# Scan loads of a hybrid encoder kernel: the shape of the DMA that fetches keys, gate rows, maxima and factors

## The chip, the cores and the metric

The kernel runs on one core of one Trainium2 chip. The metric is the device time of one execution in microseconds. The core has five engines with an instruction list each, worked through in order: PE (TensorE, matmuls; PEld is its weight load), DVE (VectorE), ACT (ScalarE), POOL (GpSimd) and SP (SyncE), which here issues nearly all DMAs. Sixteen DMA engines carry the transfers.

## What is computed

One layer of a bidirectional encoder on 2048 tokens of width 1024, in float32. Three head groups read one normalised input: neighbourhood attention (6 heads), mLSTM (4 heads of 64) and gated DeltaNet (6 heads of 64). The last two run in chunks of 64 tokens, forwards and backwards, each as a scan. Their outputs go through one projection; then follow cross-attention on 256 memory tokens, a squared-ReLU MLP and a last norm. What matters here are the two scans:

```python
# gated DeltaNet, per head and direction, chunk by chunk
def step(state, xs):
    u_c, w_c, a_c, qd_c, ks_c, gl_c = xs          # qd = q * exp(gc)
    v_new = u_c - w_c @ state
    o = qd_c @ state + a_c @ v_new
    state = state * exp(gl_c) + ks_c.T @ v_new
    return state, o

# mLSTM: m_t is the running maximum
s_intra = (q @ k.T) * exp(dmat - m_t)
a_inter = exp(inter - m_t)
num = a_inter * (q @ c_prev) + s_intra @ v
```

## The kernel before

`pass_a` projects the input and prepares the chunks: `gram` (L408) makes keys, decays and Gram matrices for 128 tokens at a time, `inv` inverts triangular blocks, `ml_prep` makes the mLSTM rows. What the scans need goes to DRAM: `kb_d` (keys times exp(gc), written at L471), `sc_d`, `v_d`, `w_d`, `gd_c`, `g_st` (cumulated gates, one row of 768 numbers for a step and direction), `mlc_d`, `mlv_d`, `mx_row` (running maxima, rows of 512) and `ai_row` (factors, rows of 512).

`pass_b` runs three generators side by side: `gdn_scan`, `ml_scan` one step later, and `heads_out`, which from the ninth mLSTM step on finishes two token tiles a step. Each scan has 16 steps of 128 tokens. A tile of 128 partitions holds both directions at once: partitions 0 to 63 and 64 to 127 (`CH`, and the swapped `SR`) belong to direction 0 at token tile m and to direction 1 at token tile 15 - m. All tiles of the scans have two buffers.

`load(m)` of `gdn_scan` (L625) fetches `wp`, `sc` (two transfers) and `qe` for each direction (L634 to L637) and then, for both directions in one transfer, `kb` (the keys) and `ge` (the gate row, the same 3 KB for each of 64 partitions), through `both` at L657. ACT takes the exponential of `ge` (L640), POOL multiplies `qe` by it into `sc` (L643), DVE writes the scaled identity into `sc` (L644), PE multiplies keys and inverses (L651), ACT copies that into `wp` (L654). A step of the scan itself is then a chain of matmul and copy: L674, L676, L681, L684, twice, with the outputs at L688 and L693 or L695.

`load(m)` of `ml_scan` (L829) fetches `mkq`, `mr_` and `mqe` by direction (L839 to L842) and, for both directions in one transfer each, `me` (the maxima, 2 KB for each of 64 partitions, L843) and `mge` (the factors, L844). DVE subtracts `me` (L845), POOL adds a mask (L846), ACT takes the exponential (L847), DVE uses it (L862); POOL uses `mge` (L866). L896 to L910 turn numerators and denominators into outputs.

In one transfer for both directions the source is a slice over the rows of a flattened (direction, token tile) axis: it takes row m and row 31 - m, so the first dimension of the source has 2 entries, and the second has 64 (rows of keys, or a repeat). The order on each engine is set by a scheduler in the framework, which plans with its own clock, so that a change of a DMA may reorder instructions near it. The names `mr__9279` and the like are the buffers of `mr_` by number.

Of the kernel before, what the change touches and what calls it, by code (L numbers as in the profile page):

```python
# [37 lines left out]
class Trunk:  # L38
# [59 lines left out]
    def mix(self):  # L98

        tc, nc, I, dr = self.tc, self.nc, self.I, self.dr  # L100
        dt = lambda name, shape: dr.tile(shape, F32, name=name)
        self.y_d = [dt(f"y_d{b}", [8, P, 512]) for b in range(4)]
        self.gd_c = dt("gd_c", [9, P, T])
        self.gate_d = dt("gate_d", [5, P, T])
        self.mlc_d = dt("mlc_d", [16, P, 4, P])
        self.mlv_d = dt("mlv_d", [16, P, 4, 65])
        self.nac_d = dt("nac_d", [6, P, T])
        self.nav_d = dt("nav_d", [T, 384])
        self.g_row = dt("g_row", [16, 2, 2, 6, 64])
        self.sc_d = dt("sc_d", [2, 16, 2, 64, 2, 6, 64])  # L110
        self.kb_d = dt("kb_d", [2, 16, 64, 2, 6, 64])
        self.g_st = dt("g_st", [2, 16, 2, 6, 64])
        self.v_d = dt("v_d", [16, 2, 64, 6, 64])
        self.x_d = dt("x_d", [384, 64, 64])
        self.w_d = [[dt(f"w_d{d}{g}", [64, 12 * (b - a), 64]) for g, (a, b) in enumerate(GROUPS)] for d in range(2)]
        self.wt_d = [dt(f"wt_d{d}", [192, 32, 32]) for d in range(2)]
        with ExitStack() as big:
            self.c = big.enter_context(self.pool("mixc", 1))
            c = self.c
            self.ind2 = self.load_const("ind2", [P, 2])  # L120
            self.gmask = self.load_const("gmask", [P, 2, 64])
            self.egl = c.tile([P, 4, 2, 2, 4, 6], F32, name="egl")
            self.rr = c.tile([P, 16, 12], F32, name="rr")
            self.gcm = c.tile([P, 2, 16, 4], F32, name="gcm")
            self.gtm = c.tile([P, 2, 16, 4], F32, name="gtm")
            self.cm = c.tile([P, 2, 16, 4], F32, name="cm")
            self.cmx = c.tile([P, 2, 16, 4], F32, name="cmx")
            self.wxx = c.tile([P, 2, 16, 4], F32, name="wxx")
            self.emt = c.tile([P, 2, 16, 4], F32, name="emt")
            self.pass_a()  # L130
            self.pass_b()
# [276 lines left out]
    def gram(self, t):  # L408

        nc, pool = self.nc, self.tp  # L410
# [3 lines left out]
        e = pool.tile([P, 2, 6, 64], F32, name="gr")  # L414
# [49 lines left out]
        for d in range(2):  # L464
            sc = pool.tile([P, 3, 6, 64], F32, name="sc")
            V.tensor_tensor(out=byp(sc[:, 0]), in0=gv[:, :, :, 0:64], in1=byp(e[:, d]), op=ALU.mult)
            V.tensor_tensor(out=sc[:, 1], in0=heads(kt), in1=col(kst[:, d]), op=ALU.mult)
            V.tensor_tensor(out=sc[:, 2], in0=heads(kt), in1=col(self.eg[:, t, d]), op=ALU.mult)
            nc.sync.dma_start(out=self.sc_d[d, t].rearrange("c s a h l -> (c s) (a h l)"), in_=sc[:, 0:2].rearrange("p a h l -> p (a h l)"))
            for c2 in range(2):  # L470
                nc.sync.dma_start(out=self.kb_d[d, t, :, c2], in_=sc[64 * c2:64 * c2 + 64, 2])  # L471

    def inv(self, g, dirs, late=False):

# [140 lines left out]
    def gdn_scan(self, pool):  # L615
# [4 lines left out]
        nc, dr = self.nc, self.dr  # L620
        V, G = nc.vector, nc.gpsimd
        CH = (slice(0, 64), slice(64, 128))
        SR = (slice(64, 128), slice(0, 64))

        def load(m):  # L625
            wp = pool.tile([P, 2, 2, 6, 64], F32, name="wp")
            sc = pool.tile([P, 2, 2, 3, 6, 64], F32, name="sc")
            kb = pool.tile([P, 2, 6, 64], F32, name="kb")
            ge = pool.tile([P, 2, 6, 64], F32, name="ge")
            qe = pool.tile([P, 6, P], F32, name="qe")  # L630
            for d in range(2):
                t = m if d == 0 else 15 - m
# [2 lines left out]
                nc.sync.dma_start(out=sc[CH[d], d, :, 0:2].rearrange("p c a h l -> p c (a h l)"), in_=self.sc_d[d, t].rearrange("c s a h l -> s c (a h l)"))  # L635
                nc.sync.dma_start(out=sc[CH[d], d, :, 2].rearrange("p c h l -> p c (h l)"), in_=self.v_d[t].rearrange("c s h l -> s c (h l)"))
                nc.sync.dma_start(out=qe[SR[d]], in_=self.gd_c[0:3, :, P * t:P * t + P].rearrange("c (h e) l -> e (c h) l", h=2))  # L637
            both(kb.rearrange("p c h l -> p (c h l)"), self.kb_d.rearrange("d t s c h l -> (d t) s (c h l)")[m:32 - m:31 - 2 * m])
            both(ge.rearrange("p c h l -> p (c h l)"), self.g_st.rearrange("d t c h l -> (d t) (c h l)")[15 - m:17 + m:2 * m + 1, None].broadcast_to([2, 64, 768]))
            nc.scalar.activation(out=ge, in_=ge, func=AF.Exp)  # L640
            for d in range(2):
                t = m if d == 0 else 15 - m
# [14 lines left out]
        def both(out, in_):  # L657

            nc.sync.dma_start(out=out, in_=in_)
# [6 lines left out]
        for m in range(16):  # L666
            nxt = load(m + 1) if m < 15 else None
            wp, sc = cur
# [148 lines left out]
    def ml_scan(self, pool):  # L817
# [11 lines left out]
        def load(m):  # L829
# [7 lines left out]
            for d in range(2):  # L837
# [2 lines left out]
                nc.sync.dma_start(out=r[CH[d], d].rearrange("p c h x -> p c (h x)"), in_=self.mlv_d[t].rearrange("(c s) h x -> s c (h x)", c=2))  # L840
                for a in range(2):
                    nc.sync.dma_start(out=qe[SR[d], a::2], in_=self.mlc_d[t, CH[a], 0:2])  # L842
            nc.sync.dma_start(out=e.rearrange("p c h l -> p (c h l)"), in_=self.mx_row.rearrange("d t c h l -> (d t) (c h l)")[m:32 - m:31 - 2 * m, None].broadcast_to([2, 64, 512]))  # L843
            nc.sync.dma_start(out=ge.rearrange("p h l -> p (h l)"), in_=self.ai_row.rearrange("d t h c l -> (d t) (h c l)")[15 - m:17 + m:2 * m + 1, None].broadcast_to([2, 64, 512]))  # L844
            V.tensor_tensor(out=e, in0=self.cmx[:, :, m, :, None].broadcast_to([P, 2, 4, 64]), in1=e, op=ALU.subtract)  # L845
            G.tensor_tensor(out=e, in0=e, in1=gm[:, None, None, :].broadcast_to([P, 2, 4, 64]), op=ALU.add)  # L846
            nc.scalar.activation(out=e, in_=e, func=AF.Exp)  # L847
# [564 lines left out]
```

## Time and profile before

| | us |
|---|---|
| median of the runs (2 runs, 4184.78 to 4187.43) | 4186.1 |
| the profiled execution | 4188.59 |
| its span, first to last instruction | 4186.8 |
| of it before the scans (0 to 985) | 985 |
| the scans (985 to 1752) | 767 |
| attention, projections, MLP (from 1752) | 2435 |

The scans' first loads are issued at about 955 us (mLSTM) and 992 us (DeltaNet); the last output tile of `heads_out` is done at 1752.03 us. PE is busy for 3492.6 us of the span (83%), DVE 1778.6, ACT 1120.4, POOL 1435.6. The granted TensorE clock is 0.903 of full speed in the mean, the lowest stretch being the scans. A stretch is read by the busy time of each engine, by who waits for what, and by the share of the 16 DMA engines that is busy.

### The profile page before, as it was taken

The page shows a single profiled execution, that of the slowest core. Times are in us where ns is not written, and L with a number is a line of the kernel's source. Part 1 is how long each engine was busy: PE and PEld are TensorE (multiplying, and loading weights), DVE is VectorE, ACT ScalarE, POOL GpSimd, SP SyncE. Part 2 cuts the span into 40 slices and gives each one's busy share as a digit, 9 for nine tenths or more (in the row PEclk, how much of TensorE's full clock was granted, in tenths as well). Part 3 has the DMA queues.
Part 4 walks back from the last instruction along what each step waited for, and adds up shares of the span by engine and source line. Part 5 has one row for each costly group of instructions (what it writes and reads, how often), then busy time and mean ns, then how long its engine had stood idle before and what let it go on. Part 6 is the DMA issues. An engine that isn't in the chain of part 4 may idle for free.

```text
span 4186.8 us, 53799 instructions
## 1 busy us (share of the span) xinstructions
PE 3492.6 (83%) x21360; PEld 2802.8 (67%) x21360; DVE 1778.6 (42%) x3241; ACT 1120.4 (27%) x1976; POOL 1435.6 (34%) x876
## 2 busy tenths in 40 slices
PE   5988999893233335499799999999999999999998
PEld 4766777673233334376578888778888877888887
DVE  7767483832133456644343434532222244222224
ACT  3222422231111111155343333422211133221122
POOL 4241523342121223211344534443333354333333
PEclk8999999895566667599899999999999999999999
DMA  4476435844243344345323233321111132111112
GB/s 132 112 212 130 137 87 168 221 105 116 89 99 94 102 116 118 134 129 158 114 86 126 96 119 131 106 78 43 46 48 48 56 101 83 43 43 48 51 51 86
DMA packets 375844, 425.24 MB, mean 102 GB/s; under 512 B 150872, under 2 KB 277544, under 8 KB 373544
## 3 DMA queue, kind: packets, MB, share of 16 engines
q1 hardware_dynamic: 375048, 420.22, 34.4%
q8 instruction: 169, 2.77, 0.3%
q0 software_dynamic: 544, 1.57, 0.2%
q14 instruction: 83, 0.68, 0.1%
HBM read 329.59 MB, written 92.12 MB: 101 GB/s over the span
## 4 chain that ended last, share of the span: by engine, by line
PE 54%; DVE 2%; issue 1%; ACT 1%; DMA 1%; POOL 1%; SPq 0%; POOLq 0%; DVEq 0%; ACTq 0%
PE psg L94 30%; PE psa L94 19%; PE psn L960 2%; PE psy L979 1%; PE pst L969 1%; DVE ss L1030 0%; PE psm L75 0%; PE psa L1198 0%; DMA xb<-x_d 0%; PE psm L85 0%; PE pst L986 0%; ACT whi L1001 0%; DMA me<-mx_row 0%; DVE gz L727 0%; POOL wlo L1003 0%
## 5 line engine op out<-in xcount | busy, mean ns | idle before, releaser
L1003 POOL TENSOR_TENSOR wlo<-wraw,whi 128x1024 fp32r<-128x1024 f32 (+2 forms) x386 | 774.4, 2007 | 1515.6 <-ACT whi L1001 1408.4
L94 PE MATMUL psg<-acta,whi 128*128 128x512 f32 (+1 forms) x3008 | 967.0, 402 | 22.4 <-ACT acta L1155 16.2
L94 PE MATMUL psg<-actb,whi 128*128 128x512 f32 x2496 | 796.5, 399 | 40.7 <-ACT actb L266 13.8
L1001 ACT CAST whi<-wraw 128x1024 fp32r<-128x1024 f32 (+2 forms) x402 | 357.6, 890 | 1217.1 <-PE psa L94 554.8
L94 PEld LDWEIGHTS psg<-acta,whi 128*128 128x128 f32 (+1 forms) x3008 | 569.4, 191 | 160.5 <-ACT acta L1155 17.5
L94 PE MATMUL psa<-ht,whi 128*128 128x512 f32 x2048 | 638.8, 395 | 0.6 <-ACT whi L1001 0.6
L94 PE MATMUL psg<-acta,wlo 128*128 128x512 f32 (+1 forms) x1504 | 602.3, 401 | 3.6 <-POOL wlo L1003 3.6
L94 PEld LDWEIGHTS psg<-actb,whi 128*128 128x128 f32 x2496 | 470.5, 190 | 156.3 <-ACT actb L266 14.6
L94 PE MATMUL psg<-actb,wlo 128*128 128x512 f32 x1248 | 499.5, 401 | 2.9 <-POOL wlo L1003 2.9
L94 PEld LDWEIGHTS psa<-ht,whi 128*128 128x128 f32 x2048 | 384.0, 188 | 94.1 <-ACT whi L1001 1.5
L94 PE MATMUL psa<-ht,wlo 128*128 128x512 f32 x1024 | 400.6, 396 | 0.5 <-POOL wlo L1003 0.5
L1247 DVE TENSOR_TENSOR fr<-fr 128x512 f32<-128x512 f32 x128 | 167.4, 1307 | 511.8 <-ACT fr L1246 511.8
L1260 DVE TENSOR_TENSOR xb<-psa,xb 128x512 f32<-128x512 f32 x256 | 175.8, 692 | 475.6 <-PE psa L94 475.6
L94 PEld LDWEIGHTS psg<-acta,wlo 128*128 128x128 f32 (+1 forms) x1504 | 286.8, 191 | 72.7 <-POOL wlo L1003 4.7
L94 PEld LDWEIGHTS psg<-actb,wlo 128*128 128x128 f32 x1248 | 236.5, 190 | 59.7 <-POOL wlo L1003 4.1
L1250 POOL TENSOR_TENSOR ht<-fr,ht 128x512 fp32r<-128x512 f32 x128 | 169.5, 1324 | 257.3 <-ACT ht L1249 254.2
L94 PEld LDWEIGHTS psa<-ht,wlo 128*128 128x128 f32 x1024 | 192.2, 188 | 48.4 <-POOL wlo L1003 1.7
L674 PE MATMUL pss<-sc,wp 128*64 128x64 f32 x768 | 48.1, 278 | 210.8 <-ACT sc L684 190.2
L674 PEld LDWEIGHTS pss<-sc,wp 128*64 128x64 f32 x768 | 40.7, 185 | 217.4 <-ACT sc L684 194.1
L681 PE MATMUL pss<-sc 128*64 128x64 f32 x744 | 53.8, 291 | 116.3 <-DVE sc L676 98.0
L301 DVE SCALAR_TENSOR_TENSOR acc<-pad,vecs,acc 128x512 f32<-128x512 f32 (+2 forms) x144 | 143.9, 1013 | 2.8
L1030 DVE TENSOR_TENSOR ss<-ss,sqt 128x512 f32<-128x512 f32 (+1 forms) x91 | 122.4, 1345 | 49.1 <-ACT sqt L1029 45.9
(383 smaller groups left out, 4141.9 us busy)
## 6 DMA issues: line engine op xcount, KB each, us to landing
wraw<-in_w_ff SPq DMA_DIRECT2D x72, 512.0 KB
wraw<-in_w_ff SPq DMA_DIRECT2D x144, 256.0 KB
wraw<-in_w_out SPq DMA_DIRECT2D x32, 512.0 KB
wraw<-in_w_xq SPq DMA_DIRECT2D x32, 512.0 KB
wraw<-in_w_xo SPq DMA_DIRECT2D x32, 512.0 KB
wraw<-in_w_gd SPq DMA_DIRECT2D x24, 512.0 KB
sc_d<-sc SPq DMA_DIRECT2D x32, 384.0 KB
sc<-sc_d SPq DMA_DIRECT2D x32, 384.0 KB
```

The source lines that it names most:

```text
L94: nc.tensor.matmul(out=out, lhsT=a(k), rhs=b(k), start=(i == 0), stop=(i == n - 1))
L301: V.scalar_tensor_tensor(out=acc[:, :n], in0=pad[:, p0 + j:p0 + j + n], scalar=cw(j), in1=acc[:, :n], op0=ALU.mult, op1=ALU.add)
L674: nc.tensor.matmul(out=ps[CH[d], 64 * h:64 * h + 64], lhsT=wp[:, d, cc[d], h], rhs=sc[:, d, cc[d], 2, h], start=True, stop=True)
L681: nc.tensor.matmul(out=ps[SR[d], 64 * h:64 * h + 64], lhsT=sc[:, d, cc[d], 1, h], rhs=sc[:, d, cc[d], 2, h], start=True, stop=True)
L960: nc.tensor.matmul(out=sp[:, :nk], lhsT=q[hb, hp], rhs=grid(ks)[hb, hp, r0:r0 + nr, c0:c0 + ncl], start=True, stop=True)
L969: nc.tensor.transpose(out=tp[:n, P * j:P * j + P], in_=s[:, kt * j:kt * j + n], identity=self.ident)
L1001: nc.scalar.copy(out=hi, in_=raw)
L1003: (lo_eng or nc.gpsimd).tensor_tensor(out=lo, in0=raw, in1=hi.bitcast(F32), op=ALU.subtract)
L1030: nc.vector.tensor_tensor(out=ss, in0=ss, in1=sq, op=ALU.add)
L1247: V.tensor_tensor(out=r, in0=r, in1=r, op=ALU.mult)
L1250: G.tensor_tensor(out=ht[:, 1], in0=r, in1=ht[:, 0].bitcast(F32), op=ALU.subtract)
L1260: V.tensor_tensor(out=xs[nb][:, j], in0=ps, in1=xs[nb][:, j], op=ALU.add)
```

## The change

`kb_d` is laid out by step and then direction, so that the two 64-row blocks of a step lie behind one another, and the load reads them as 128 rows of 768 numbers: one first dimension of 128. The loads of `ge`, `me` and `mge` are cut in two, one for each direction, each from one row repeated over 64 partitions: a first dimension of 64 in place of 2. The bytes moved stay the same. A step issues 23 loads in place of 20.

```diff
-        self.kb_d = dt("kb_d", [2, 16, 64, 2, 6, 64])
+        self.kb_d = dt("kb_d", [16, 2, 64, 2, 6, 64])
...
-                nc.sync.dma_start(out=self.kb_d[d, t, :, c2], in_=sc[64 * c2:64 * c2 + 64, 2])
+                nc.sync.dma_start(out=self.kb_d[15 - t if d else t, d, :, c2], in_=sc[64 * c2:64 * c2 + 64, 2])
...
-            both(kb.rearrange("p c h l -> p (c h l)"), self.kb_d.rearrange("d t s c h l -> (d t) s (c h l)")[m:32 - m:31 - 2 * m])
-            both(ge.rearrange("p c h l -> p (c h l)"), self.g_st.rearrange("d t c h l -> (d t) (c h l)")[15 - m:17 + m:2 * m + 1, None].broadcast_to([2, 64, 768]))
+            both(kb.rearrange("p c h l -> p (c h l)"), self.kb_d[m].rearrange("d s c h l -> (d s) (c h l)"))
+            for d in range(2):
+                nc.sync.dma_start(out=ge[SR[d]], in_=self.g_st[1 - d, 15 - m if d else m][None].broadcast_to([64, 2, 6, 64]))
...
-            nc.sync.dma_start(out=e.rearrange("p c h l -> p (c h l)"), in_=self.mx_row.rearrange("d t c h l -> (d t) (c h l)")[m:32 - m:31 - 2 * m, None].broadcast_to([2, 64, 512]))
-            nc.sync.dma_start(out=ge.rearrange("p h l -> p (h l)"), in_=self.ai_row.rearrange("d t h c l -> (d t) (h c l)")[15 - m:17 + m:2 * m + 1, None].broadcast_to([2, 64, 512]))
+            for d in range(2):
+                t = m if d == 0 else 15 - m
+                nc.sync.dma_start(out=e[CH[d]], in_=self.mx_row[d, t][None].broadcast_to([64, 2, 4, 64]))
+                nc.sync.dma_start(out=ge[SR[d]].rearrange("p h l -> p (h l)"), in_=self.ai_row[1 - d, t].rearrange("h c l -> (h c l)")[None].broadcast_to([64, 512]))
```

The order on SP before, in the loads around the seventh `ge` (`x2` is two of a kind in a row, the sizes are those written in SBUF):

```order
L637 DMA qe<-gd_c 64x6x128 x2
L659 DMA kb<-kb_d 128x1x768
L659 DMA ge<-g_st 128x1x768
L842 DMA mqe<-mlc_d 64x2x128
L844 DMA mge<-ai_row 128x1x512
L839 DMA mkq<-mlc_d 128x512 x2
L843 DMA me<-mx_row 128x1x512
L634 DMA wp<-w_d_85 64x768
L634 DMA wp<-w_d_90 64x768
```

The same place after, where the lines stand one to three lines further down in the file:

```order
L637 DMA qe<-gd_c 64x6x128 x2
L660 DMA kb<-kb_d 128x768
L640 DMA ge<-g_st 64x768 x2
L841 DMA mr__9551<-mlv_d 64x2x260 x2
L843 DMA mqe<-mlc_d 64x2x128 x4
L847 DMA mge<-ai_row 64x512 x2
L634 DMA wp<-w_d_85 64x768
L634 DMA wp<-w_d_90 64x768
L840 DMA mkq<-mlc_d 128x512 x2
L846 DMA me<-mx_row 64x512 x2
```

Three of the four loads are two instructions now and `kb` is one with a first dimension of 128; `mr_` and `mqe` of the mLSTM step have moved in behind `ge`, and `wp` of the next DeltaNet step ahead of `mkq` and `me`. On DVE, before, the stretch from the eighth subtraction of `me` on:

```order
L845 TENSOR_TENSOR me<-cmx,me 128x512
L896 COPY den<-psl 128x4
L897 SCALAR_TENSOR_TENSOR ab<-den 128x4
L900 TENSOR_TENSOR ab<-ab,emt 64x4 x2
L901 RECIPROCAL ab<-ab 128x4
L906 TENSOR_TENSOR acc<-psl,ab 64x256 x2
L684 COPY sc<-pss 64x384
L644 TENSOR_TENSOR sc<-ident,egl 64x2x384 x2
L693 COPY acc<-pss 64x384
```

The same stretch after:

```order
L848 TENSOR_TENSOR me<-cmx,me 128x512
L645 TENSOR_TENSOR sc<-ident,egl 64x2x384 x2
L694 COPY acc<-pss 64x384
L677 COPY sc<-pss 64x384
L891 COPY mr__9293<-psl 64x260
L899 COPY den<-psl 128x4
L900 SCALAR_TENSOR_TENSOR ab<-den 128x4
L903 TENSOR_TENSOR ab<-ab,emt 64x4 x2
L904 RECIPROCAL ab<-ab 128x4
L909 TENSOR_TENSOR acc<-psl,ab 64x256 x2
```

DVE still has the subtraction of `me` ahead of the copies of both scans; the scaled identity (L644, now L645) and two copies of the DeltaNet scan have moved ahead of the denominators (L896 to L901, now L899 to L904).

## Rows read from the trace of the kernel before

**Rows 1.** Busy time by stretch: engines, granted PE clock, DMA share, GB/s.

```profile
core 0: us, PE busy (x) PEld busy (x) DVE busy (x) ACT busy (x) POOL busy (x), PEclk, DMA share, GB/s
985.00:1755.00 770.00, 285.32 (x4776) 253.35 (x4776) 331.73 (x734) 110.89 (x220) 185.26 (x119) 0.63 0.38 105
...
1143.50:1150.30 6.80, 0.00 (x0) 0.00 (x0) 0.00 (x0) 0.00 (x0) 0.00 (x0) 0.50 0.13 51
...
1151.00:1479.00 328.00, 122.59 (x2208) 111.42 (x2208) 118.67 (x221) 50.11 (x104) 70.02 (x46) 0.65 0.37 97
...
1415.00:1745.00 330.00, 143.19 (x2398) 125.00 (x2396) 202.47 (x475) 53.94 (x104) 99.51 (x63) 0.67 0.38 105
...
1702.00:1724.20 22.20, 9.57 (x122) 7.92 (x122) 16.17 (x50) 2.24 (x5) 3.87 (x2) 0.65 0.20 60
```

**Rows 2.** Waits, 985 to 1755 us: us in total, times, longest us.

```profile
ACT ge L640 <- DMA ge<-g_st: 290.6, 16, 27.4
...
DVE me L845 <- DMA me<-mx_row: 235.9, 14, 49.1
```

**Rows 3.** Timeline: start us, us, engine, what [idle before <- releaser]; a gate row's load.

```profile
1137.81 0.52 SPq L659 DMA_DIRECT2D ge<-g_st  x1
...
1150.84 0.84 ACT L640 ACTIVATE ge<-ge 128x768 f32<-128x768 f32 x1 [15.22 <-DMA ge<-g_st]
1151.59 0.46 ACT L684 COPY sc<-pss 64x384 f32<-64x384 f32 x1
...
1152.10 0.38 PE L674 MATMUL pss<-sc,wp 128*64 128x64 f32 x2 [12.92 <-ACT sc L684]
```

**Rows 4.** Timeline of DVE: where it stops, from one `me` to the next.

```profile
1201.42 0.69 DVE L845 TENSOR_TENSOR me<-cmx,me 128x512 f32<-128x512 f32 x1 [32.79 <-DMA me<-mx_row]
...
1236.66 0.56 DVE L693 COPY acc<-pss 64x384 f32<-64x384 f32 x1 [19.78 <-ACT acc L693]
...
1250.18 0.69 DVE L845 TENSOR_TENSOR me<-cmx,me 128x512 f32<-128x512 f32 x1 [10.37 <-DMA me<-mx_row]
```

**Rows 5.** Timeline of `gram`: broadcast rows loaded one row per transfer.

```profile
676.34 2.42 SPq L416 DMA_DIRECT2D gr<-g_row  x4
...
680.77 0.96 DVE L435 TENSOR_TENSOR gr<-gr,gcg 128x768 f32<-128x768 f32 x1 [12.87 <-DMA gr<-g_row]
...
682.37 2.11 DVE L435 TENSOR_TENSOR gr<-gr,gcg 128x768 f32<-128x768 f32 x1 [0.64 <-DMA gr<-g_row]
```

**Rows 6.** Timeline of the first DeltaNet step: the first gate row and first scan matmul.

```profile
1002.41 0.63 SPq L659 DMA_DIRECT2D ge<-g_st  x1
...
1026.68 0.84 ACT L640 ACTIVATE ge<-ge 128x768 f32<-128x768 f32 x1 [24.15 <-DMA ge<-g_st]
...
1045.26 1.55 PE L674 MATMUL pss<-sc,wp 128*64 128x64 f32 x24
```

**Rows 7.** Tile and line views: count, duration ns min/median/max, first and last start us.

```profile
L640 ACT ACTIVATE ge<-ge x8: 842/842/843, 1194.0 to 1479.0; 128x768 f32<-128x768 f32 x8
...
L643 POOL TENSOR_TENSOR sc<-qe,ge x32: 1794/1848/2603, 1027.6 to 1614.7; 64x768 f32<-64x768 f32 x32
...
L659 SPq DMA_DIRECT2D ge<-g_st x16: 517/526/3783, 1002.4 to 1570.6; - x16
...
L901 DVE RECIPROCAL ab<-ab x32: 160/178/179, 1002.2 to 1739.1; 128x4 f32<-128x4 f32 x32
...
L644 DVE TENSOR_TENSOR sc<-ident,egl x32: 950/1222/2574, 993.3 to 1617.8; 64x768 f32<-64x768 f32 x32
```

**Rows 8.** Waits of SP's queue, 985 to 1755 us: total, times, longest us.

```profile
SPq L637 <- POOL sc L643: 69.0, 10, 14.3
...
SPq L634 <- PE pss L674: 48.2, 5, 15.2
```

**Rows 9.** Groups by line, 985 to 1755 us: busy us, mean ns, idle before.

```profile
L644 DVE TENSOR_TENSOR sc<-ident,egl 64x768 f32<-64x768 f32 x32 | 49.6, 1552 | 3.4 <-DMA w_d<-m 2.6 <-issue 0.3
...
L900 DVE TENSOR_TENSOR ab<-ab,emt 64x4 f32<-64x4 f32 x64 | 26.1, 409 | 1.3
```

## Prediction

> **What bounds the kernel now.** I read the share of PE by slices first: PE is nearly full except in the scans, so I took the table of stretches. From 985 to 1755 us no engine is half busy: DVE 331.73 of 770 us, PE 285.32, POOL 185.26, and the 16 DMA engines 0.38 in the mean [rows 1]. So something late holds all of them. The list of waits names it: ACT stood 290.6 us for the 16 gate rows `ge`, DVE 235.9 us for the maxima `me` [rows 2]. Both engines work in order, so what stands behind waits too: when `ge` came at 1150.84, after 15.22 us, ACT could make its copy of `sc`, and only then could PE start the next L674, idle for 12.92 us [rows 3]. On DVE it is alike: from one `me` at 1201.42 to the next at 1250.18, 48.76 us, it waits 19.78 + 10.37 us [rows 4], so its own work there is about 18.6 us.
>
> Why are these loads late? In the stretch 1143.5 to 1150.3 no engine runs and the gate row alone is on its way: the DMA share is 0.13 and the rate 51 GB/s [rows 1]. 2 of 16 is 0.125. The load, whose first dimension is 2, is carried by two DMA engines at about 25 GB/s each. At 51 GB/s, 384 KB (`kb`, `ge`) take 7.7 us each and 256 KB (`me`, `mge`) 5.1 us each, 25.6 us a step for the four, all on those two. A step takes (1479.0 - 1194.0)/7 = 40.7 us [rows 7]; at a share of 0.37 [rows 1] that is 0.37 x 16 x 40.7 = 241 us of engine time a step. Without the four (2 x 25.6 = 51) 190 us are left, 11.9 for each engine. The two engines thus have 25.6 + 11.9 = 37.5 of 40.7 us to do, the other fourteen 11.9. The two are the bound of the scans, and every other load of the step has 1/16 of its bytes behind them.
>
> **The change, part by part.** (1) The first dimension of `kb` becomes 128, that of `ge`, `me`, `mge` 64. If each is spread over 16, the 241 us a step come to 15.1 per engine. That such a load of one row spreads, `gram` shows: four loads `gr` of 192 KB, one row for 64 partitions each, are issued from 676.34 on; DVE takes the first pair at 680.77 and the second at 682.37 [rows 5], 768 KB in 6.0 us, while the same bytes on two engines would take 15.4 us. I take 4 us from issue to use for a pair, where the load of both halves in one took 13 [rows 3]. (2) Three more issues a step, 48 in all, at the median of 526 ns [rows 7]: 25 us of SP's time. A step's 23 issues make 12.1 us of SP, under the period that follows below, so I count them at nothing; if SP were the bound it would be 25 us. Behind the new second halves stand `mqe` and `wp`, later by 0.5 us each. (3) The store of `kb_d` writes as many rows of the same length to another place: nothing, with a bound of a few us either way. (4) The order on DVE is mixed a little differently; I count nothing and leave 1 us a step either way, 16 us in all, to the range.
>
> What is late next? Each step in its first half (m below 8) has 18.6 us of DVE's work as it stands between the waits [rows 4], PE's 122.59 us for 328 us, 15.2 a step at the present clock [rows 1], DMA's 15.1, SP's 12.1. DVE is the fullest. It gives 18.6 and I add 2.4 for waits of the copy chain: 21 us. The lower end is 16, where DMA and PE fill it and DVE's stretched operations shrink; the upper 28 (second rival). In the second half `heads_out` joins. From 1415 to 1745 DVE is busy 202.47 us, 25.3 a step [rows 1]. At 1702 to 1724.2 one mLSTM step with its two output tiles runs without any load to wait for: 22.2 us, DVE busy 16.17 [rows 1]. The DeltaNet step adds the other 25.3 - 16.2 = 9.1 us of DVE's work, part of which fits into the 6 us idle there: between 25.3 and 22.2 + 9.1 = 31.3; I take 29, nearer to the upper end, since the chain of copies is in order.
>
> The start: `ge` of the first step is issued at 1002.41 and used at 1026.68, and the first scan matmul comes at 1045.26 [rows 6]. With `kb` and `ge` there at 1006.5, then 0.84 for the exponential, two multiplies of 1.85 on POOL [rows 3, 7] and the copies of `wp`, I set the first scan matmul at 1015. The end: after the last DeltaNet step one mLSTM step with outputs, 22.2 us [rows 1], and the last two tiles, which now take from 1739.1, the last reciprocal [rows 7], to 1752: 13 us.
>
> Sum: 1015 + 8 x 21 + 8 x 29 + 35 = 1450 us as the end of the scans in place of 1752: 302 us less. What follows from 1752 on does not change; its first loads are issued behind the scans' last, as now. 4188.59 - 302 = 3886.6 for the profiled execution; the runs' median lies 2.5 below it, so **3884 us**, 7.2% faster.
>
> Two rules of the Trainium skill stand beside this. The trace shows a pair of half loads in 4 us [rows 5] against 13 for one load of both halves [rows 3]. The Trainium skill, page "DMA: Bandwidth & Descriptors", section "Rules for kernel authors", says the contrary of what is done to three of the loads: two transfers to disjoint halves of the partitions are not worth it, they serialise. By that rule only `kb` would gain; this is the third rival. The second concerns DVE. L644 takes 950 ns at least and 1552 in the mean [rows 7, 9], and L900, on 4 columns, 409 ns where the reciprocal on 4 columns takes 178 [rows 7, 9]. POOL is busy 185.26 of 770 us now [rows 1] and would be for 185 of 465. The stretching of L644 and L900 alone, 32 x 0.60 + 64 x 0.25 = 35 us, would grow to 35 x 0.40/0.24 = 58: 23 us, for which the range has room. The Trainium skill, page "SBUF — State Buffer", section "SBUF: two separate sides", gives a cause: an operation of DVE with two inputs from SBUF and one of POOL that reads SBUF block each other wholly. By it the sum would be 3907.
>
> **The rivals.** *A new wait in the old one's place.* SP issues in order and waits for buffers: 69.0 us behind POOL's L643, 48.2 behind L674 [rows 8], 7.3 us a step for these two. If they stay, and loads come that much later than needed, a step is 18.6 + 7.3 + 2 = 28 in the first half, 25.3 + 9 = 34 in the second: 1015 + 224 + 272 + 35 = 1546, 206 less, **3980 us**. For it: a buffer is free only when a whole step is done with it. Against: L643 itself waits for `ge`, so the 69 us are mostly the same lateness.
>
> *All the way to the floors.* 16 us and 25.3 us a step: 1015 + 128 + 202 + 35 = 1380, 372 less, **3814 us**. For it: PE's clock is 0.65 of full in the scans and 0.50, the lower level of 1.2 GHz, where it idles [rows 1]; a denser PE may be granted more of 2.4 GHz. Against: 16 is below DVE's 18.6.
>
> *The halves stay slow.* If the halves of `ge`, `me` and `mge` go one after the other at the old rate, only `kb` spreads: the two engines lose 7.7 us a step and gain 1.0, 34.0 in place of 40.7. From 1002.4 to 1570.6 the loads set the pace [rows 7], 14 steps: 94 us less, 25 us more for issues: **4117 us**, within 2%. This is also about what is left if the change does not spread them as it says. Against: [rows 5].
>
> *One row too hot.* Slower than before: sixteen engines read the same 2 or 3 KB at once. If DRAM gives one row at no more than the 25 GB/s that each engine draws now, a half load of `ge` takes 7.7 us and one of `me` or `mge` 5.1, one after another, now on all engines: 2 x 7.7 + 4 x 5.1 = 35.8 a step, and 13 for the rest: 48.8 in place of 40.7. Over 14 steps 113 us more: **4299 us**. It decides below about 33 GB/s a row. For it: nothing shows a row read by 16 engines at such a density. Against: the `gr` loads, four rows one after the other at 768 KB in 6.0 us, 130 GB/s [rows 5].
>
> **How the numbers follow.** The forecast 0.60, the new wait 0.20, the floors 0.15, the halves that stay slow 0.04, the hot row 0.01. A measurement of this kernel tells about 2%, 84 us, from no change: faster by more 0.95, within 0.04, slower 0.01. The range goes from the floors, 3814, to the new wait, 3980, with a few us beyond each for the order on DVE: 3805 to 3990. That leaves the third and fourth rival outside, and some of the tails.
>
> **What would show it.** In the profile after: the wait of ACT for `ge` and of DVE for `me` under 50 us each instead of 290.6 and 235.9; from issue to use of a gate row 4 to 6 us; steps of `ge` about 21 us apart in the first half and 29 in the second; DMA share of the scans about 0.6 to 0.7, and no stretch at 0.13; the end of `heads_out` at about 1450, and nothing else moved by more than 15 us. DVE should be busy over 70% of the scans. The prediction is wrong if `ge` still takes over 10 us, if SP shows waits of as many us as now, or if the first half's step stays above 28 us.

## The result, and the profile after

The changed kernel takes 3910.49 us (median of 2 runs, 3909.13 to 3911.84) against 4186.1: a ratio of 0.9342 with a 95% interval of 0.9301 to 0.9382, 276 us less. The forecast was 3884 in a range of 3805 to 3990, faster by over 2% with a chance of 0.95. The profiled execution took 3911.84 us, its span is 3910.1, against 4188.59 and 4186.8.

The page of the changed kernel: the first line of busy times, then the clock granted to PE and the DMA share in 40 slices of 97.8 us, then the main DMA queue (packets, MB, share of 16 engines).

```profile
PE 3484.4 (89%) x21360; PEld 2794.2 (71%) x21360; DVE 1781.4 (46%) x3241; ACT 1120.5 (29%) x1976; POOL 1435.7 (37%) x876
...
PEclk8999999998677767999999999999999999999999
DMA  4466533875866625552232333211111141111112
...
q1 hardware_dynamic: 376698, 420.22, 37.7%
```

The engines do the work they did (DVE 1781.4 us against 1778.6); what is gone is idle time, and it is gone from the scans, as the line views show. They give count, duration in ns (min/median/max), first and last start. First the kernel before: the scan's first matmul L674, the copies into `acc` of the first eight steps (L693), the additions of the last eight (L695), and the last gate of `heads_out` (L727).

```profile
L674 PE MATMUL pss<-sc,wp x768: 219/314/369, 1045.3 to 1663.9; 128*64 128x64 f32 x192
...
L693 DVE COPY acc<-pss x16: 549/552/561, 1104.7 to 1421.6; 64x384 f32<-64x384 f32 x16
...
L695 DVE TENSOR_TENSOR acc<-pss,acc x32: 542/554/562, 1427.7 to 1675.7; 64x384 f32<-64x384 f32 x32
...
L727 DVE SCALAR_TENSOR_TENSOR gz<-psl,hnw,gz x80: 334/343/352, 1500.2 to 1751.7; 128x128 f32<-128x128 f32 x80
```

The same four lines of the changed kernel, one line further down in its text:

```profile
L675 PE MATMUL pss<-sc,wp x768: 219/304/369, 998.3 to 1394.5; 128*64 128x64 f32 x192
...
L694 DVE COPY acc<-pss x16: 549/552/561, 1011.4 to 1200.7; 64x384 f32<-64x384 f32 x16
...
L696 DVE TENSOR_TENSOR acc<-pss,acc x32: 537/555/562, 1206.0 to 1398.2; 64x384 f32<-64x384 f32 x32
...
L728 DVE SCALAR_TENSOR_TENSOR gz<-psl,hnw,gz x80: 333/344/352, 1263.2 to 1472.5; 128x128 f32<-128x128 f32 x80
```

The four starts cut the scans into pieces that add up: the start, the first half (eight steps up to the last copy), the second half (up to the last addition), and the tail of the mLSTM scan and its outputs.

| | before | forecast | after |
|---|---|---|---|
| first scan matmul at | 1045.3 | 1015 | 998.3 |
| first half, a step | 47.0 | 21 | 25.3 |
| second half, a step | 31.8 | 29 | 24.7 |
| tail | 76.0 | 35 | 74.3 |
| end of `heads_out` | 1751.7 | 1450 | 1472.5 |

So 47 us are gained at the start, 174 in the first half, 57 in the second, 2 in the tail: 279 us. What follows the scans is as long as it was, within 3 us.

The busy time by stretch, with the granted PE clock, the DMA share and GB/s as the last three columns; first the three pieces of the kernel before, to which [rows 1] gave no row cut like this:

```profile
1045.30:1421.60 376.30, 129.69 (x2238) 117.89 (x2238) 114.91 (x216) 55.17 (x113) 76.27 (x50) 0.62 0.36 95
1421.60:1675.70 254.10, 113.49 (x2026) 99.82 (x2022) 144.47 (x314) 43.60 (x86) 77.05 (x49) 0.69 0.42 114
1675.70:1751.70 76.00, 27.91 (x312) 22.90 (x312) 56.02 (x167) 7.74 (x13) 20.28 (x12) 0.59 0.32 109
```

and the changed kernel, the whole of its scans and then its three pieces:

```profile
core 0: us, PE busy (x) PEld busy (x) DVE busy (x) ACT busy (x) POOL busy (x), PEclk, DMA share, GB/s
985.00:1478.00 493.00, 268.48 (x4722) 238.21 (x4718) 326.55 (x712) 110.28 (x218) 179.13 (x116) 0.70 0.63 157
...
998.30:1200.70 202.40, 119.61 (x2260) 107.62 (x2258) 118.70 (x225) 53.77 (x111) 77.15 (x52) 0.74 0.73 180
1200.70:1398.20 197.50, 112.45 (x2024) 99.98 (x2024) 152.36 (x324) 45.60 (x90) 77.77 (x51) 0.71 0.60 147
1398.20:1472.50 74.30, 27.93 (x312) 23.00 (x312) 55.12 (x164) 7.01 (x12) 20.27 (x12) 0.59 0.33 113
```

In the first half the same work (some 2240 matmuls, 220 instructions of DVE) is done in 202 us instead of 376, and the DMA rate goes from 95 to 180 GB/s. In the tail nothing has changed: 74.3 us against 76.0, with the same work.

The list of waits between 985 and 1478 us, engine, line and what it waited for, us in total, times, longest; it answers to [rows 2], and the SP lines below to [rows 8]:

```profile
ACT ge L641 <- DMA ge<-g_st: 94.1, 15, 12.0
DVE me L848 <- DMA me<-mx_row: 84.1, 13, 20.7
...
SPq L637 <- POOL sc L644: 30.2, 10, 7.9
...
SPq L634 <- PE pss L675: 18.6, 5, 5.8
```

The waits for the gate row and the maxima are a third of what they were (290.6 and 235.9), not gone. A gate row in the timeline of the changed kernel (start, duration, engine; in brackets the idle time before and what ended it), to be laid beside [rows 3]:

```profile
1107.72 1.25 SPq L640 DMA_DIRECT2D ge<-g_st  x2
...
1111.96 0.84 ACT L641 ACTIVATE ge<-ge 128x768 f32<-128x768 f32 x1 [7.28 <-DMA ge<-g_st]
1112.71 0.46 ACT L685 COPY sc<-pss 64x384 f32<-64x384 f32 x1
```

From issue to use the pair takes 4.24 us, where one load of both halves took 13.03; and yet ACT stood idle for 7.28 us before it: 3 of them before the pair was issued at all. This pair is the quickest; over the sixteen pairs it is 4.2 to 9.9 us from issue to use, 6.9 in the median.

### The profile page after: what moved, and what is told of

It is laid out like the page before. It is cut to its first block, busy times and chain, and to the rows that moved or that the text cites. A ratio compares the mean times of both kernels' runs of the same rounds, so it can differ in the third digit from the quotient of the medians.

```text
span 3910.1 us, 53847 instructions
## 1 busy us (share of the span) xinstructions
PE 3484.4 (89%) x21360; PEld 2794.2 (71%) x21360; DVE 1781.4 (46%) x3241; ACT 1120.5 (29%) x1976; POOL 1435.7 (37%) x876
## 4 chain that ended last, share of the span: by engine, by line
PE 60%; DVE 7%; DMA 6%; POOL 3%; issue 2%; SPq 2%; ACT 1%; POOLq 0%; DVEq 0%; ACTq 0%
PE psg L94 33%; PE psa L94 20%; PE psn L963 2%; PE psy L982 2%; PE pst L972 1%; DMA me<-mx_row 1%; DMA ge<-g_st 1%; DVE tv L493 1%; DVE x L494 1%; POOL sc L644 1%; POOL x L494 0%; DMA qe<-gd_c 0%; POOL wlo L1006 0%; DMA y_d<-gz 0%; DMA x<-x_d 0%
## 5 line engine op out<-in xcount | busy, mean ns | idle before, releaser
L94 PEld LDWEIGHTS psa<-ht,wlo 128*128 128x128 f32 x1024 | 192.2, 188 | 48.8 <-POOL wlo L1006 2.7
L1252 ACT CAST ht<-fr 128x512 fp32r<-128x512 f32 x128 | 79.6, 622 | 179.8 <-DVE fr L1250 179.7
L1249 ACT ACTIVATE fr<-psg 128x512 f32<-128x512 f32 x128 | 76.1, 594 | 140.6 <-PE psg L94 140.6
```

Of the source, the lines that this page charges most:

```text
L94: nc.tensor.matmul(out=out, lhsT=a(k), rhs=b(k), start=(i == 0), stop=(i == n - 1))
L1249: S.activation(out=r, in_=ps, func=AF.Relu)
L1252: S.copy(out=ht[:, 0], in_=r)
```

## The experiments

Theory: the four loads were late because two DMA engines carried all of them; a load's first dimension decides how many engines carry it; after the change the traffic of all loads over sixteen engines holds the first half. The rivals come with each run. "A step" is a step of the first half, read as above.

**Each part alone** (all start from the kernel before).

Keys only:

```diff
-        self.kb_d = dt("kb_d", [2, 16, 64, 2, 6, 64])
+        self.kb_d = dt("kb_d", [16, 2, 64, 2, 6, 64])
...
-            both(kb..., self.kb_d.rearrange("d t s c h l -> (d t) s (c h l)")[m:32 - m:31 - 2 * m])
+            both(kb..., self.kb_d[m].rearrange("d s c h l -> (d s) (c h l)"))
```

> Only the keys are stored by step and loaded as 128 rows; the gate row, maxima and factors are fetched as before, first dimension 2. Theory (two DMA engines carry these loads and set the step): 7.7 us a step leave the two engines, 1 us comes back spread, at 37.5 of 40.7 us busy that is a step of about 33 us over some 14 steps, 108 us less: 4078 us. Rival (the longest waits decide): the keys stand for only 31 us of PE's waits, so no more than about 30 us less: 4156 us.

Gate row only, the line of `ge` as in the change:

```diff
-            both(ge..., self.g_st...[15 - m:17 + m:2 * m + 1, None].broadcast_to([2, 64, 768]))
+            for d in range(2):
+                nc.sync.dma_start(out=ge[SR[d]], in_=self.g_st[1 - d, 15 - m if d else m][None].broadcast_to([64, 2, 6, 64]))
```

> Only the gate row of the DeltaNet scan is fetched by direction. Theory: the same 7.7 us a step as for the keys, for the two loads have the same bytes: 4078 us, the same as with the keys alone within 30 us. Rival (the longest waits decide): ACT waited 290.6 us for this load, so most of the whole gain of 276 us is here: below 4000 us.

Maxima and factors only, the lines of `me` and `mge` as in the change:

```diff
-            nc.sync.dma_start(out=e..., in_=self.mx_row...broadcast_to([2, 64, 512]))
-            nc.sync.dma_start(out=ge..., in_=self.ai_row...broadcast_to([2, 64, 512]))
+            for d in range(2):
+                nc.sync.dma_start(out=e[CH[d]], in_=self.mx_row[d, t][None].broadcast_to([64, 2, 4, 64]))
+                nc.sync.dma_start(out=ge[SR[d]]..., in_=self.ai_row[1 - d, t]...broadcast_to([64, 512]))
```

> Only maxima and factors of the mLSTM scan are fetched by direction. Theory: 10.3 us a step leave the two engines, a step of about 30.3 us: 146 us less, 4040 us. Rival (the longest waits decide): the maxima stand for 235.9 us of DVE's waits, the factors for little; but the DeltaNet scan still waits for its gate row, so that under 60 us are gained: above 4126 us. By the theory the three parts alone sum to more than the whole (362 against 276), as another bound takes over at a step of 25 us.

Measured, one run each beside 4187.64 for the kernel before: 4106.6, 4104.27 and 4079.82, that is 81, 83 and 108 us less. Each is 26 to 40 us short of the theory's number. I had expected the three parts to add up to more than the whole; they add up to it, 272 us against 276. The gate row, on whose load ACT waited longest, is worth no more than the keys, for which PE waited 31 us in all. It is the bytes taken off two engines that count, not who is seen to wait. The steps say how: 41.0 us with the keys spread, 39.8 with the gate row, 38.2 with maxima and factors, from 47.0. Taking 7.7 us off two engines and giving back an eighth of it over sixteen should save 6.7; it saved 6.0 and 7.2. For maxima and factors, 10.2 us, it should save 8.9; it saved 8.8. The three together 22.4, and the whole change saved 21.7.

**The first dimension, or the cutting in two?** The changed kernel with the halves of `ge`, `me` and `mge` written with a first dimension of 2, then of 4:

```diff
-                nc.sync.dma_start(out=e[CH[d]], in_=self.mx_row[d, t][None].broadcast_to([64, 2, 4, 64]))
+                nc.sync.dma_start(out=e[CH[d]]..., in_=self.mx_row[d, t]...[None, None].broadcast_to([2, 32, 512]))
```

> The kernel after, but each load of a gate row, of maxima and of factors by direction is written with a first dimension of 2 (2 x 32 repeats) in place of 64; keys as after. Same bytes, same count of loads, one row each. Theory (the first dimension sets the number of engines): these loads are on two engines again, as with the keys alone: 4060 to 4110 us, and the waits for gate row and maxima come back to over 150 us each. Rival (it is the cut by direction, or one row per load, that helps): as after, 3910 us.

> As e4_dim2 with a first dimension of 4 (4 x 16 repeats). Theory: four engines carry 9 us a step of these loads beside their 12 to 13 us of the rest, 22 us, below the step of about 25 us that the kernel after has: 3915 to 3990 us. Rival (only all sixteen engines help): half way between two engines and sixteen, above 4000 us.

Measured 4120.52 (beside 4187.64; 10 us above the theory's range, and far from the rival) and 3982.99 (beside 4189.5; at the upper end of the theory's range). With 2, the waits for gate row and maxima are back at 203.9 and 208.6 us, as expected. The same bytes in the same number of transfers to the same partitions: 4120.5, 3983.0 and 3910.5 us for 2, 4 and 64 rows in the first dimension, and steps of 41.4, 30.8 and 25.3. On four engines the other three loads' 17.9 us become 9.0: 47.0 - 6.7 - 9.0 = 31.3, measured 30.8. With 2, only the keys' gain is left, and the step is that of the run with the keys alone (41.0). One stretch of the run with 2, the first half:

```profile
1023.00:1354.00 331.00, 125.69 (x2258) 113.73 (x2258) 117.81 (x225) 55.01 (x112) 77.59 (x52) 0.63 0.44 112
```

A DMA share of 0.44 with 331 us for the work that takes 202: two engines are the bound, while the mean looks idle. The engines can be counted, too. Cut into slices of 1 us, the first half of the kernel before has a DMA share of 0.11 to 0.14, two sixteenths, in 178 of 376 slices (48 GB/s in their mean). With 2 rows it is 105 of 331 slices; the changed kernel has 3 of 202. With 4 rows there are 4 such slices of 246, but 36 with a share of 0.23 to 0.27, four sixteenths, at 90 GB/s.

**The keys' layout, or their first dimension?** Keys stored as before, and loaded by direction, 64 rows each:

```diff
-            both(kb..., self.kb_d[m].rearrange("d s c h l -> (d s) (c h l)"))
+            for d in range(2):
+                nc.sync.dma_start(out=kb[CH[d]]..., in_=self.kb_d[d, 15 - m if d else m].rearrange("s c h l -> s (c h l)"))
```

> The kernel after with the keys stored as before and loaded by direction, two loads of 64 rows, one more issue a step. Theory: the layout of the store is worth nothing by itself, the first dimension of 64 spreads as well as 128; one issue of 0.5 us a step is hidden: 3910 us within 0.5%. Rival (SP's queue is on the path): 16 x 0.6 = 10 us more or above, 3920 to 3940 us.

Measured 3905.13 (3903.26 to 3911.91, 4 runs), ratio 0.933 with an interval of 0.9315 to 0.9346: the changed kernel's time. The new layout in DRAM is worth nothing by itself, 64 rows spread as 128 do, and one more issue a step costs nothing that can be measured.

**What holds the step after?** First DVE: the changed kernel with the scaled identity built on POOL.

```diff
-                V.tensor_tensor(out=sc[SR[d], d, :, 1], in0=self.ident[...]...
+                G.tensor_tensor(out=sc[SR[d], d, :, 1], in0=self.ident[...]...
```

> The kernel after with the scaled identity of the DeltaNet scan written by POOL in place of DVE. It takes 49.6 us of DVE's busy time away and adds about 32 x 1.1 = 35 us to POOL. If DVE's own work is the bound: 30 to 50 us less, 3860 to 3880 us. If it is DMA or the chain of copies: within 10 us of 3910 us; if POOL's chain (mask, factors, gate) becomes the bound: slower, 3920 to 3960 us.

Measured 3905.67, a step 24.9. In the changed kernel's groups by line the operation moved is this one (busy us and mean ns of one, then idle before it):

```profile
L645 DVE TENSOR_TENSOR sc<-ident,egl 64x768 f32<-64x768 f32 x28 | 41.0, 1463 | 0.7 <-issue 0.3
```

Its first half, to be laid beside the row 998.30:1200.70 above:

```profile
998.80:1198.00 199.20, 117.48 (x2242) 106.07 (x2242) 96.39 (x216) 53.47 (x110) 95.17 (x68) 0.73 0.74 183
```

41 us of DVE's work taken away and 5 us gained, which one run does not tell from nothing; in the first half DVE is busy for 96 us instead of 119, and the stretch is as long. So DVE's own work is not the bound there, on whose 18.6 us my forecast of the step stood.

Then the loads. All four once, at step 0, and the first step's rows used in every step (this leaves the other fifteen steps' keys, gate rows, maxima and factors out of the computation):

```diff
+        nc.sync.dma_start(out=kb..., in_=self.kb_d[0]...)
+        for d in range(2):
+            nc.sync.dma_start(out=ge0[SR[d]], in_=self.g_st[1 - d, 15 if d else 0]...)
...
-            nc.scalar.activation(out=ge, in_=ge, func=AF.Exp)
+            nc.scalar.activation(out=ge, in_=ge0, func=AF.Exp)
```

> Keys, gate row, maxima and factors are fetched once, for step 0, and used for all 16 steps: the loads of the other 15 steps are left out (exponentials and products remain, on the wrong numbers). What is left of the scans is what the four loads do not hold. Theory A (DVE's own work and the copy chain are the next bound, as forecast): the first half's step stays above 21 us and no more than 50 us are gained on the kernel after: 3860 to 3910 us. Theory B (the DMA engines, busy 0.70 of the first half, still set the step): 56 of 277 us of engine time a step go, a fifth, the first half's step falls from 24.7 towards 19 us, and 60 to 120 us are gained: 3790 to 3850 us.

Measured 3807.79, in theory B's range: 103 us less than the changed kernel, a step 18.0. Its first half:

```profile
987.40:1131.70 144.30, 103.88 (x2299) 93.58 (x2298) 112.89 (x214) 54.28 (x111) 76.91 (x51) 0.88 0.74 171
```

Without these loads DVE is busy for 78% of the stretch, PE 72%, at a granted clock of 0.88 (0.74 in the changed kernel, 0.62 before; PE does the same matmuls in 104, 120 and 130 us). But several things went together here: the traffic, the waits of ACT and DVE for it, and seven issues of SP a step. The twin run was meant to separate them: everything is loaded twice, the second time into tiles that nothing reads.

```diff
+            both(kbx..., self.kb_d[m].rearrange("d s c h l -> (d s) (c h l)"))
+            for d in range(2):
+                nc.sync.dma_start(out=gex[SR[d]], in_=self.g_st[1 - d, 15 - m if d else m]...)
...
+                nc.sync.dma_start(out=ex[CH[d]], in_=self.mx_row[d, t]...)
+                nc.sync.dma_start(out=gex[SR[d]]..., in_=self.ai_row[1 - d, t]...)
```

> The changed kernel, and each step loads the keys, gate rows, maxima and factors a second time, into tiles that nothing reads: 1.25 MB more a step and 7 issues (3.7 us of SP), nobody waits for it. It tells apart the two things that went together in the run that loads them once (first half 18.0 us a step instead of 25.3): the traffic, and the waits of ACT and DVE for it. Theory (the DMA engines' traffic holds the first half): the step grows by about what it fell there, 7.3 us, to 30 to 33 us, and the kernel takes 3950 to 4020 us. Rival (what was saved there is the waiting, the engines have room at a share of 0.70): the step stays at 24 to 27 us and the kernel at 3900 to 3930 us.

Measured 3964.93 (3961.69 to 3967.64, 4 runs), ratio 0.9472, interval 0.9456 to 0.9488; a step 31.4:

```profile
995.80:1246.80 251.00, 127.31 (x2250) 113.93 (x2248) 123.49 (x217) 53.87 (x109) 83.54 (x55) 0.66 0.95 223
```

The step grew as the theory said, but for a larger dose. As no engine waits for the second loads, SP issues them ahead of the scan, and the last is issued before the second half begins at 1246.8. Two of their tile views (start of the first and the last):

```profile
L665 SPq DMA_DIRECT2D kbx<-kb_d x16: 325/580/585, 972.3 to 1203.7; - x16
...
L857 SPq DMA_DIRECT2D mex<-mx_row x32: 444/592/602, 952.2 to 1227.4; - x32
```

So the first half carried 14 of the 16 second loads of the keys, 28 of 32 of the gate row and 60 of 64 of maxima and factors: 18.9 MB, 2.36 a step where 1.31 were meant (the 1.25 of the expectation, which counts in units of 1024 x 1024 bytes). And the second half carried none, so that its 25.0 us a step against 24.7 say nothing.

What the run does show is this. The sixteen engines at their fullest (slices of 1 us with a share of 0.95 or more, 173 of 251) moved 244 GB/s; at that rate 2.36 MB are 9.7 us, and the step grew by 6.1: part of the added traffic found room, the rest cost time. The run that loads them once took 11.4 MB out of its first half, 5.7 us a step at the changed kernel's fullest rate of 249 GB/s, and gave back 7.3. So adding and taking away do not mirror each other, and the traffic alone does not account for what was given back. How much of it was traffic and how much the waits stays open.

SP's issues changed with both runs, too (188 in the changed kernel's first half, 294 and 122 in these), and SP stood for some of the second loads to land before it could issue the next into the same tile. Counted at 0.526 us they fill 12.4 and 19.3 us of steps of 25.3 and 31.4, so SP is not the fullest; that they cost nothing here is not shown.

**Is it bytes, or only the moment of issue?** Three edits that leave the bytes alone. The four loads issued a step earlier, with a third buffer for each tile:

```diff
+        def fetch(m):
+            kb = pool.tile([P, 2, 6, 64], F32, name="kb", bufs=3)
+            ge = pool.tile([P, 2, 6, 64], F32, name="ge", bufs=3)
...
+            after = fetch(m + 1) if m < 15 else None
             nc.scalar.activation(out=ge, in_=ge, func=AF.Exp)
```

> The changed kernel, but keys, gate rows, maxima and factors of step m+2 are issued one step earlier, behind the other loads of step m+1, with a third buffer for each of the four tiles. Bytes, issues and layouts are as in the changed kernel (3908 us). Theory (the first half's step of 24.7 us is DMA engine time, 277 us over 16 engines = 17.3 us an engine, plus the lag of a step's loads behind each other): the same bytes have to be moved, only their place in the queue changes, so 3890 to 3915 us. Rival (the loads come late because they are issued late): the waits for ge (94 us) and me (84 us), of which about half lies on the chain, go: 3840 to 3875 us.

A third buffer for `kb`, `ge`, `qe`, `me` and `mge`, the order as it is:

```diff
-            kb = pool.tile([P, 2, 6, 64], F32, name="kb")
+            kb = pool.tile([P, 2, 6, 64], F32, name="kb", bufs=3)
```

> The changed kernel with three buffers instead of two for kb, ge, qe, me and mge; order of issues unchanged. The prediction's rival of a new wait (SP held for a buffer, 30.2 us behind POOL's L644 and 18.6 us behind L675 between 985 and 1478) says that these waits make the loads late: 3865 to 3890 us. Theory (the SP waits are lateness of the same chain and cost nothing by themselves): 3900 to 3915 us, and SP then waits for the buffers that are still two (sc, wp, msc).

The halves of `ge` and `me` issued from ACT's queue:

```diff
-                nc.sync.dma_start(out=ge[SR[d]], ...)
+                nc.scalar.dma_start(out=ge[SR[d]], ...)
```

> The changed kernel with the gate-row and maxima halves (4 loads a step) issued from ACT's queue instead of SP's; ACT stands at them in its own order, and SP has 4 x 0.53 us less a step. If the order of issues on SP's queue (12 us of issuing a step) made these loads late: 3870 to 3895 us. Theory: SP's issuing is covered, and a load behind ACT's copies is issued no earlier: 3905 to 3950 us.

Measured, four runs each: 3897.45 (3896.06 to 3899.34; ratio 0.9302, 0.9288 to 0.9316), 3907.92 (3906.41 to 3910.58; 0.9327, 0.9313 to 0.9341) and 3898.66 (3893.07 to 3908.94; 0.9306, 0.9284 to 0.9327). The first half's steps are 25.4, 24.9 and 24.3, against 25.3. With the loads a step earlier, the first half reads:

```profile
989.40:1192.50 203.10, 123.79 (x2293) 111.16 (x2292) 114.40 (x209) 54.64 (x110) 77.09 (x51) 0.73 0.79 192
```

ACT's wait for the gate row over all of the scans fell, from 94.1 us to 56.2. In the first half it did not; first the changed kernel (998.3 to 1200.7), then this one (989.4 to 1192.5):

```profile
ACT ge L641 <- DMA ge<-g_st: 54.3, 8, 10.3
...
ACT ge L646 <- DMA ge<-g_st: 53.0, 10, 10.4
```

The eighth gate row, the pair of 1107.72 in the changed kernel, shows why:

```profile
1071.77 1.11 SPq L630 DMA_DIRECT2D ge<-g_st  x2
...
1078.46 0.84 ACT L646 ACTIVATE ge<-ge 128x768 f32<-128x768 f32 x1 [4.94 <-DMA ge<-g_st]
```

Its issue came 36 us earlier and the exponential 34, while the scan itself began 9 us earlier: the exponential moved ahead with its load, and ACT stood for the loads as long as before. So the run does not take the waits away, and the rival (the waits are the price) is not refuted by it; it says only that these bytes, a step earlier, cost the same step. What this version gains, 11.1 us at the end of `heads_out`, comes from the first matmul (989.4 instead of 998.3) and, 2.9 us, from what follows the first half. All four of its runs lie below both of the changed kernel's, 13 us in the median, but the two intervals overlap: it may be a little better, and it is not told apart from the run with ACT's queue. With three buffers SP still waits for POOL at the same place, 25.8 us where it was 30.2, and nothing is gained:

```profile
SPq L637 <- POOL sc L644: 25.8, 6, 7.1
```

The run with ACT's queue fell between its two expectations (3895 and 3905), and its interval, 3889 to 3907 us, reaches into both: it decides nothing. In its first half the waits for gate row and maxima were shorter, 35.2 and 39.1 us where the changed kernel has 54.3 and 59.0, and the stretch fell by 8 us.

## Why the prediction was right, and which of its terms were not

**Right: what bound the kernel.** The two engines that carry four loads are the cause of what the first half gained. The doses (2, 4, 64 rows) and the three parts, each within some 1 us a step of the engine time it moves, show it, and so does the count of engines in the slices of 1 us. With hindsight the step after follows from that alone: 47.0 - 25.6 x 7/8 = 24.6 us, measured 25.3. One thing is left over. By the share of 0.36 the other loads fill 13.7 us a step of each engine, so that the two have 25.6 + 13.7 = 39.3 of 47.0 us to do, and the runs do not show what fills the rest.

**Mis-sized: the first half, 25.3 us a step and not 21 (+34 us in eight).** The prediction asked which engine is the fullest once the two are relieved, and answered with DVE, 18.6 + 2.4. Three terms were off. DVE's 18.6 came from one stretch of 48.76 us [rows 4] with 36 of DVE's instructions, where the first half has 27 a step:

```profile
1201.42:1250.18 48.76, 20.15 (x352) 18.52 (x352) 17.22 (x36) 7.59 (x16) 10.65 (x7) 0.64 0.46 111
```

Read as PE's 15.2 was read, DVE's share of the same row [rows 1] gives 118.67/328 x 40.7 = 14.7 us, below PE's and DMA's terms; the changed kernel has 14.8. "DMA's 15.1" was too small. It rested on a step of 40.7 us read from the gate rows' exponentials between 1194.0 and 1479.0 [rows 7]. These run ahead of the scan and straddle its two halves, whose own steps were 47.0 and 31.8. At 47.0 the engine time is 0.36 x 16 x 47.0 = 271 us a step, not 241; after the change it is 0.73 x 16 x 25.3 = 295 us, 18.5 for each engine. And the 2.4 us for waits was too small beside either, as the waits for the four loads did not go. What sets the step after is not shown: not DVE's own work (the run with POOL), and not full engines alone, as all sixteen are busy in only 87 of 202 slices of 1 us.

**Second half and tail: right in the sum, wrong in the cut.** The forecast had 8 x 29 + 35 = 267 us for the two, measured 271.8. Singly they were 24.7 a step and not 29 (-34 us), and 74 and not 35 (+39 us). The step that failed is the lag of the mLSTM scan. The prediction let one step of it follow the last DeltaNet step (L695, 1675.7), as the program's order has it; the trace of before has three, two reciprocals each:

```profile
L901 DVE RECIPROCAL ab<-ab x6: 177/178/178, 1693.9 to 1739.1; 128x4 f32<-128x4 f32 x6
```

So the 202.47 us of DVE between 1415 and 1745, from which 25.3 a step was worked out, run on through 69 us of the tail, with three mLSTM steps in it; in the changed kernel's second half itself DVE is busy for 19.0 us a step. That 24.7 lies near 25.3 is chance. The lag is not fixed either: with the identity on POOL four reciprocals are left and the tail is 49.3 us, with the loads a step earlier it is 99.5, so only the sum of the two pieces can be compared. That sum in the changed kernel, with the identity on POOL, and with the four loads made once:

```profile
1200.70:1472.50 271.80, 140.39 (x2336) 122.98 (x2336) 207.48 (x487) 52.61 (x102) 98.05 (x63) 0.68 0.53 138
...
1198.00:1464.80 266.80, 140.61 (x2352) 121.94 (x2346) 190.60 (x467) 52.30 (x101) 113.78 (x75) 0.69 0.52 140
...
1131.70:1371.00 239.30, 137.65 (x2382) 119.33 (x2382) 203.97 (x496) 51.80 (x99) 99.75 (x63) 0.73 0.50 135
```

DVE's work went down by 17 us and the time by 5; without the loads it went down by 32 us with DVE's work nearly as before. So DVE is not the bound here by itself, and what is was not shown.

**Too careful: the start, 998.3 and not 1015 (-17 us).** The prediction kept the first issue at 1002.41 [rows 6]. But SP issues the mLSTM scan's first loads ahead of it, and in the kernel before SP was held at them. The first `mkq`, before and after:

```profile
956.09 3.01 SPq L839 DMA_DIRECT2D mkq<-mlc_d  x1
...
956.83 0.58 SPq L840 DMA_DIRECT2D mkq<-mlc_d  x1
```

From the first `me` to the first `ge` SP needed 47.5 us before (954.91 to 1002.41) and 20.7 after (954.39 to 975.08), so the first exponential is now at 984.9, in the tile view of `ge`:

```profile
L641 ACT ACTIVATE ge<-ge x16: 843/844/847, 984.9 to 1308.7; 128x768 f32<-128x768 f32 x16
```

The four errors, +34, -34, +39 and -17, add up to +22 us, and the forecast was 26.5 short. That the time came so near is in part luck: the middle two are one error that cancels itself, and the start makes up for half of the first half.

**The signs.** Gate row from issue to use in 4 to 6 us: in part, 4.2 to 9.9, 6.9 in the median. Waits under 50 us each: wrong, 94.1 and 84.1; SP's waits fell from 69.0 and 48.2 to 30.2 and 18.6. DMA share 0.63: as forecast. No stretch at 0.13: 3 slices of 202 are left of 178. The end of `heads_out` at about 1450: 1472.5. DVE over 70%: wrong, 326.55 of 493, 66%.

**The rivals.** The new wait at SP's buffers: the two waits came to 48.8 us, not to the 117 of before, and the 3980 us did not come. Three buffers did not take these waits away, so the run with them (3907.9) does not price them. The floors, 3814: not reached as long as the four loads are made in every step; with them made once the step is 18.0 us and the kernel takes 3807.79. The halves that stay slow, 4117: that is what was measured when the halves had 2 rows first (4120.5). So the Trainium skill's rule that the prediction set against the change (page "DMA: Bandwidth & Descriptors", section "Rules for kernel authors": two transfers to disjoint halves serialise, do not bother) does not carry over to this case. The page gives as its reason that both halves are spread over all sixteen engines and so share them; here the whole used two and the halves more, and the measurement decides: the gate row alone cut in two took 4104.27 us, maxima and factors 4079.82. Another rule of the same section holds in this case: an outermost dimension smaller than 16, such as a leading repeat, confines the whole transfer to at most that many engines; 4120.5, 3983.0 and 3910.5 us for 2, 4 and 64 agree. The hot row, 4299: nothing of it, with every pair used within 9.9 us of its issue and the kernel faster.

**Open.** What sets the step after the change. The mean DMA share is 0.73, the loads come in bursts, more traffic costs time and less gives it back; but in none of the runs did the traffic stay and the waits of ACT and DVE for the four loads go altogether, or the other way round. The other loads (`sc`, `wp`, `mkq`) were not moved, and whether that would shorten the step was not tried.

## What to carry to other kernels

Before reading a low mean DMA share as room, look for a stretch in which one transfer is alone and see how many sixteenths it fills (0.13 is two engines); then the loads' bytes on those engines, not the list of waits, say what spreading them is worth. In this kernel the first dimension of a DMA's access pattern set how many engines carried it (2, 4 or many more), and a larger one could be had by splitting a transfer or by storing its source in the order of use. For the time after, take the step from an operation of the scan itself and subtract what leaves the two engines (here 47.0 - 22.4); that came within 1 us here, and nothing says that another bound cannot come first elsewhere. Where two scans run side by side, count in the trace how far one lags. And before reading a run with added or moved loads, see in its trace where the loads really went.

## What the runs showed that I had not expected

With all sixteen engines busy, the loads of these scans moved 249 GB/s in the changed kernel and 244 with everything loaded twice (slices of 1 us with a share of 0.95 or more), 15 to 16 GB/s an engine, where two engines on a lone gate row drew 25.5 each. Averaged over a first half the rate per busy engine is 95/(0.36 x 16) = 16.5 GB/s before, 15.4 in the changed kernel, 14.7 with the loads twice and 14.4 with them once: well below 25.5 in all, and not in the order of the traffic. So engine time worked out from a lone transfer is too short where many are under way. And PE's granted clock rose with its density: 0.62, 0.74 and 0.88 of full in the first half, between the levels of 1.2 and 2.4 GHz, where PE was busy for 34%, 59% and 72% of it, so that the same matmuls took 26 us less in the last than in the first.
